# A two-layer conv and attention trunk: layer 1's up projections in seven products of halves, attention in steps of two query blocks

## The chip, the cores and the metric

The kernel runs on one core of a Trainium2 chip. The metric is the device time of one execution in microseconds (us). The engines named below are TensorE (PE in the profile, with PEld for its weight loads), VectorE (DVE), ScalarE (ACT), GpSimd (POOL) and SyncE (SP, which issues DMAs).

## What is computed

The input is 512 tokens of 1024 values in float32. Layer 0 is a causal convolution module (projection and gate, 31 taps per channel, a norm over channels, projection) and a SwiGLU feed-forward block of width 2816. Keys and values are then projected once. Layer 1 is attention (16 heads of 64, four key heads, a window of 128 tokens, a position bias and a sink per head) and a second feed-forward block. A last RMSNorm ends it. The parts that matter here:

```python
def swiglu_ffn(x, w_up, w_down):
    gate, up = jnp.split(x @ w_up, 2, axis=-1)
    return (jax.nn.silu(gate) * up) @ w_down

h = h + attn @ w_o[j]
h = h + swiglu_ffn(rmsnorm(h, norm_ffn[l]), ffn_w_up[l], ffn_w_down[l])
```

In attention each block of 128 queries sees its own block of keys and the one before.

## The kernel before

Values stand channels first: the residual h is eight tiles of 128 channels x 512 tokens. A float32 product is made in three passes (mm3, L268 to L274): every operand is split into a rounded high part and a low remainder, and high x high, high x low and low x high are added up in a PSUM bank. There are eight banks, and bank() (L176) takes the next.

**The weight stream.** Weights come in chunks of 128 x 1024 (512 KB) in the order of PLAN. load (L194) issues their DMAs on SP into four raw buffers; advance (L202) splits them three chunks ahead of their use: a cast on ScalarE to the high part whi and a subtraction on VectorE to the low part wlo (both L214), with four buffers each. get (L254) hands a chunk out.

**The feed-forward block of layer 1.** Its 22 column tiles of gate and up are taken in 11 pairs. A pair (ffn_up, L518) uses four chunks (two halves of the 1024 inputs, gate and up), eight tiles of 128 x 128 each, in three passes over all 512 tokens: 96 matmuls into four banks. evac (L522, L553 to L556) multiplies by the reciprocal norm on VectorE, takes SiLU on ScalarE, multiplies gate by up on GpSimd and splits the result (L430, L431). After the pairs of one part come its down chunks (down_group, L449), 24 matmuls each, and four residual additions per group (L514). The parts are pairs 0 to 5, 6 to 8 and 9 to 10 (HALVES1, LAST); the last part's down products are made token block by token block, from L1156 on. The normalised input comes from Next.on_h (L602): each finished tile of h is multiplied by its gain and split (L426, L427), and its square is added to a sum on GpSimd (Rms.add, L377 to L383).

**Attention.** query (L1020) projects a quarter of the queries. unit (L1040) does two pairs of heads for one block of 128 queries, in stages: scores (one tiny matmul at L1053, then L1057), bias, sink and maximum on VectorE (L1060), exponential on ScalarE (L1067), division on GpSimd (L1071), transposes (L1079) with copies to SBUF (L1081), weighted values (L1088), split (L1094, L1095). pipeline (L1098) has 20 steps over 16 units; each step works on up to four units, and query and the first half of the output projection call a step after each few matmuls. The position bias of all heads stands in one tile, filled by eight DMAs (read_bias, L957). The output projection's second half runs after it, and its residual additions (L1130) feed Next.on_h.

The order of each engine's queue is set by a scheduler from a modelled timeline in which the program's order gives priority; issue_after adds an order by hand. [...] The functions that change:

## Time and profile before

| | |
|---|---|
| median of 3 runs | 1094.72 us (1093.32 to 1095.68) |
| profiled execution | 1092.52 us |
| its span | 1090.7 us |
| granted TensorE clock | 0.999 |
| 580.9 to 720.5 us of the span | queries, attention, output projection |
| 720.5 to 1058.6 us | layer 1's feed-forward block, but for the last down products |

In a row of the timeline stand the start in us from the span's start, the duration, the engine, the line, the operation, what it writes and reads with shapes, how often (x), and in brackets the idle time before it and what ended it. A group's row has the count behind the x, then the busy time in us, the mean of one in ns, and the idle time before the group's instructions. A row of the chain has a start, a duration and the work that the end waited for.

### The profile page before, as it was taken

What the parts mean: (1) busy time and instruction counts of PE and PEld (TensorE: products, weight loads), DVE (VectorE), ACT (ScalarE), POOL (GpSimd) and SP (SyncE); (2) the same over time, 40 slices, a digit from 0 to 9 for tenths busy, and PEclk for the clock granted to TensorE, in tenths of its full rate; (3) what the DMA queues carried; (4) which work ended last, traced back from release to release, by engine and by line L of the source; (5) the groups of instructions that cost most, each with busy time, mean ns of one, the idle gap of its engine ahead of it and who ended that gap; (6) DMA issues with size and microseconds to landing.
All of it is one profiled execution on the core that took longest, in us unless ns stands there. A gap on an engine that the chain in (4) does not pass through costs nothing.

```text
span 1090.7 us, 14781 instructions
## 1 busy us (share of the span) xinstructions
PE 1083.0 (99%) x5514; PEld 910.6 (83%) x5514; DVE 636.8 (58%) x1042; ACT 492.6 (45%) x891; POOL 329.8 (30%) x430
## 2 busy tenths in 40 slices
PE   9999999999999999999999999999999999999997
PEld 8888889999888888888888766788888888888886
DVE  3999988977777554443474666484544333444353
ACT  3887888664655332322353555253322211232233
POOL 3999997710322111110120433050211100111010
PEclk9999999999999999999999999999999999999999
DMA  9247045575566423323222111222222232332212
GB/s 359 75 106 89 20 151 197 183 241 183 186 181 190 142 85 110 96 98 99 97 82 97 58 40 42 90 98 81 97 97 97 97 98 97 97 97 97 97 37 78
DMA packets 39555, 124.39 MB, mean 114 GB/s; under 512 B 4251, under 2 KB 10556, under 8 KB 39484
## 3 DMA queue, kind: packets, MB, share of 16 engines
q1 hardware_dynamic: 38764, 122.36, 35.4%
q10 hardware_dynamic: 720, 1.10, 0.3%
q8 instruction: 43, 0.70, 0.3%
q14 instruction: 28, 0.23, 0.1%
HBM read 118.20 MB, written 5.24 MB: 113 GB/s over the span
## 4 chain that ended last, share of the span: by engine, by line
PE 98%; issue 1%; DMA 0%; POOL 0%; ACT 0%; SPq 0%; POOLq 0%; DVE 0%
PE bank L272 23%; PE bank L273 23%; PE bank L274 23%; PE bank L669 10%; PE bank L304 5%; PE bank L270 4%; PE bank L305 3%; PE bank L1166 2%; PE bank L1088 1%; PE bank L1057 1%; PE bank L1079 1%; PE bank L767 1%; PE bank L657 1%; DMA both<-in_lead_dram 0%; PE bank L419 0%
## 5 line engine op out<-in xcount | busy, mean ns | idle before, releaser
L272 PE MATMUL bank<-quad,whi 128*128 128x512 f32 (+1 forms) x1200 | 440.5, 368 | 0.0
L274 PE MATMUL bank<-quad,wlo 128*128 128x512 f32 (+1 forms) x1200 | 439.1, 366 | 0.0
L273 PE MATMUL bank<-quad,whi 128*128 128x512 f32 (+1 forms) x1200 | 439.0, 366 | 0.0
L214 DVE TENSOR_TENSOR wlo<-raw,whi 128x1024 fp32r<-128x1024 f32 x186 | 258.1, 1388 | 303.8 <-ACT whi L214 299.4
L214 ACT CAST whi<-raw 128x1024 fp32r<-128x1024 f32 x186 | 195.1, 1049 | 326.5 <-PE bank L273 275.1
L272 PEld LDWEIGHTS bank<-quad,whi 128*128 128x128 f32 x1200 | 226.3, 189 | 40.7 <-issue 3.6
L273 PEld LDWEIGHTS bank<-quad,whi 128*128 128x128 f32 x1200 | 226.4, 189 | 37.0 <-issue 1.6
L274 PEld LDWEIGHTS bank<-quad,wlo 128*128 128x128 f32 x1200 | 226.3, 189 | 36.7 <-issue 0.6
L556 POOL TENSOR_TENSOR tmp<-tmp,tmp 128x512 f32<-128x512 f32 x34 | 48.1, 1417 | 408.7 <-DVE tmp L555 393.4
L711 POOL TENSOR_TENSOR pr<-pr,pr 128x256 f32<-128x256 f32 x208 | 156.7, 789 | 7.3 <-ACT pr L710 7.1
L718 DVE SCALAR_TENSOR_TENSOR bank<-apad,wdw,bank 128x256 f32<-128x256 f32 x248 | 112.5, 485 | 3.4
L710 ACT ACTIVATE pr<-apad,wdw 128x256 f32<-128x256 f32 x208 | 98.2, 501 | 14.8 <-POOL pr L711 12.9
L669 PE MATMUL bank<-quad,w 128*128 128x256 f32 x448 | 98.7, 380 | 0.0
L669 PEld LDWEIGHTS bank<-quad,w 128*128 128x128 f32 x448 | 84.9, 190 | 11.8 <-issue 0.2
L383 POOL TENSOR_TENSOR tmp<-tmp,tmp 128x256 f32<-128x256 f32 (+1 forms) x35 | 38.6, 1104 | 154.2 <-ACT tmp L379 117.3
L304 PE MATMUL bank<-quad,whi 128*128 128x512 f32 x212 | 75.9, 398 | 0.0
L554 ACT ACTIVATE tmp<-tmp 128x512 f32<-128x512 f32 x34 | 21.4, 632 | 93.0 <-DVE tmp L553 93.0
L305 PE MATMUL bank<-quad,wlo 128*128 128x256 f32 x212 | 59.3, 280 | 0.0
L1071 POOL TENSOR_SCALAR sc<-sc,sm 128x256 f32<-128x256 f32 (+1 forms) x64 | 32.9, 533 | 71.2 <-DVE sm L1069 71.2
L304 PEld LDWEIGHTS bank<-quad,whi 128*128 128x128 f32 x212 | 39.7, 188 | 8.4
L555 DVE TENSOR_TENSOR tmp<-bank,rsbc 128x512 f32<-128x512 f32 x34 | 23.5, 691 | 32.4 <-PE bank L274 32.4
L1067 ACT ACTIVATE sc<-sc,m 128x257 f32<-128x257 f32 (+1 forms) x64 | 30.2, 473 | 26.4 <-DVE m L1060 20.8
(166 smaller groups left out, 937.5 us busy)
## 6 DMA issues: line engine op xcount, KB each, us to landing
raw<-in_W_dram SPq DMA_DIRECT2D x198, 512.0 KB, 3.5
w<-in_W_dram SPq DMA_DIRECT2D x14, 512.0 KB, 9.6
fd<-fs SPq DMA_DIRECT2D x1, 3072.0 KB, 34.2
h<-in_xT_dram SPq DMA_DIRECT2D x8, 256.0 KB, 8.4
bias<-fd SPq DMA_DIRECT2D x8, 256.0 KB, 5.8
both<-in_lead_dram SPq DMA_DIRECT2D x3, 512.0 KB, 6.0
out_dram<-hg SPq DMA_DIRECT2D x4, 256.0 KB, 2.0
out_dram<-hg ACTq DMA_DIRECT2D x4, 256.0 KB, 2.3
```

What stands on the lines that cost most here:

```text
L214: latest[:] = [nc.scalar.copy(hi, r).ins, lo_engine[0].tensor_sub(lo, r, f32(hi)).ins]
L270: nc.tensor.matmul(out, w[0], x, start=start, stop=stop)
L272: nc.tensor.matmul(out, w[0], x[0], start=start, stop=False)
L273: nc.tensor.matmul(out, w[0], x[1], start=False, stop=False)
L274: nc.tensor.matmul(out, w[1], x[0], start=False, stop=stop)
L304: nc.tensor.matmul(first[2], first[0], first[1], start=start, stop=False)
L305: nc.tensor.matmul(second[2], second[0], second[1], start=False, stop=stop)
L556: nc.gpsimd.tensor_mul(t2, t1, t2)
L669: mm = nc.tensor.matmul(self.pb[:, w * W2:(w + 1) * W2], w1_of(ct, w, k), x[k] if x else xg[k][:, tok], start=k == 0, stop=k == KT - 1)
L710: on_act = nc.scalar.mul(pr, a[:, j:j + W2], tap(j))
L711: on_pool = nc.gpsimd.tensor_add(pr, acc, pr)
L718: on_dve = nc.vector.scalar_tensor_tensor(yt if i == nd - 1 else c, src, tap(i), c if i else self.shift, op0=ALU.mult, op1=ALU.add)
```

## The change

Layer 1's up projections are made by Strassen's method. Weights of a pair are cut in two column tiles and two halves of the inputs, activations in two halves of the inputs and two halves of the tokens, and seven products of halves replace eight. The sums of weights (S1 to S4) are made on GpSimd from the raw chunks and split like a chunk; three pieces (A11, A12, A22) are split directly, gate and up apart. A piece is 1024 columns wide and has 24 matmuls of 256 tokens. The sums of activations (T1 to T4) are made once, by class Rows, while the output projection ends. Products are put together in an SBUF tile (c) by VectorE, GpSimd and ScalarE, before the reciprocal norm. Layer 1 has parts of 4, 3, 2 and 2 pairs instead of 6, 3 and 2. Attention takes two blocks of queries in a step, ten steps instead of twenty; on TensorE each step's matmuls are chained (scores, weighted values, transposes), and the bias stands in tiles by four heads, three buffers, the last filled in the third query. Low parts of weights go behind the last bias operation on VectorE.

```diff
-HALVES1 = ((0, 6), (6, 9))
+HALVES1 = ((0, 4), (4, 7), (7, 9))
...
+SEVEN = ("A11 B11", "S3 T3", "S1 T1", "S2 T2", "A12 B21", "S4 B22", "A22 T4")
+SEVEN_FIRST = ("A11 B11", "S1 T1", "S3 T3", "S2 T2", "A12 B21", "S4 B22", "A22 T4")
...
+def slot_plan(plan):
+
+    slots = []
+    for i, c in enumerate(plan):
+        if c[0] != "up" or not by_seven(c[1], c[2]):
+            slots.append((i, None))
+        elif c[3:] == (0, 0):
+            slots += [(i + (3 if n else 1), (c[1], c[2], n)) for n in range(7)]
+    return slots
...
+    def split_weights(hi, lo, src):
+        on_act = nc.scalar.copy(hi, src).ins
+
+        with tc.issue_after(biased[0]) if biased[0] else nullcontext():
+            latest[:] = [on_act, lo_engine[0].tensor_sub(lo, src, f32(hi)).ins]
...
+    def seven_sources(layer, pair, n):
+
+        name = order_of(layer, pair)[n].split()[0]
+        if name[0] == "S":
+            sums[name] = sums_pool[0].tile([P, 2, 4, P], F32, tag="sum", name=uid("sum"), bufs=4)
+        out = []
+        for which in range(2):
+            a = {f"A{m + 1}{half + 1}": raws[AT["up", layer, pair, half, which]].rearrange("p (k m c) -> p m k c", k=4, m=2)[:, m]
+                 for half in range(2) if n or not half for m in range(2)}
+            if name in a:
+                out.append(a[name])
+                continue
+            s = {k: v[:, which] for k, v in sums.items()}
+            if name == "S1":
+                nc.gpsimd.tensor_add(s[name], a["A21"], a["A22"])
+            elif name == "S2":
+                nc.gpsimd.tensor_sub(s[name], s["S1"], a["A11"])
+            elif name == "S3":
+                nc.gpsimd.tensor_sub(s[name], a["A11"], a["A21"])
+            else:
+                nc.gpsimd.tensor_sub(s[name], a["A12"], s["S2"])
+        return out or [sums[name].rearrange("p a k c -> p (a k c)")]
...
+        load(SLOTS[min(len(SLOTS) - 1, u + SPLIT_AHEAD - 1)][0] + 1 + DMA_AHEAD - SPLIT_AHEAD)
+        while stream["split"] < min(len(SLOTS), u + SPLIT_AHEAD):
+            n = stream["split"]
+            i, blocks = SLOTS[n]
...
+            if blocks is None:
+                split_weights(hi, lo, raws.pop(i))
+                continue
+            src = seven_sources(*blocks)
+            if len(src) == 1:
+                split_weights(hi, lo, src[0])
+                continue
+            for e in range(2):
+                split_weights(*(w[:, e * 512:(e + 1) * 512].rearrange("p (k c) -> p k c", k=4) for w in (hi, lo)), src[e])
...
-        hid = ffn_up(layer, lo, hi, xg, tok, rms, twin, plain)
+        hid = ffn_up7(layer, lo, hi, xg, pool7) if layer else ffn_up(layer, lo, hi, xg, tok, rms, twin, plain)
...
+    class Rows:
+
+
+        def __init__(self, gain):
+            self.gain = gain
+            self.rms = Rms(new_bc(), ALL)
+            self.x = [quad(F32) for _ in range(2)]
+            self.block = {}
+
+        def part(self, name, k, src):
+
+            if name not in self.block:
+                self.block[name] = quads.tile([P, 2, 4, 256], F32R, tag="quad", name=uid("rows"))
+            split([self.block[name][:, a, k:k + 2, :] for a in range(2)], src)
+
+        def on_h(self, i):
+            nc.scalar.mul(self.x[i // 4][:, i % 4, :], h[i], col(self.gain, i))
+            if i < 4:
+                self.rms.add(h[i])
+            if i % 2 == 0:
+                return
+            k = i % 4 - 1
+            b11, b12, b21, b22 = (x[:, k:k + 2, s] for x in self.x for s in HALF)
+            if i < 4:
+                self.part("B11", k, b11)
+                t1 = temp().rearrange("p (k s) -> p k s", k=2)
+                nc.vector.tensor_sub(t1, b12, b11)
+                self.part("T1", k, t1)
+                return
+
+            nc.vector.tensor_sub(b12, b22, b12)
+            self.part("T3", k, b12)
+            nc.vector.tensor_add(b11, b12, b11)
+            self.part("T2", k, b11)
+            self.part("B21", k, b21)
+            if i < 7:
+                return
+            for j in range(4, KT):
+                self.rms.add(h[j])
+            for k in (0, 2):
+                self.part("B22", k, self.x[1][:, k:k + 2, HALF[1]])
+            for k in (0, 2):
+
+                t4 = self.x[1][:, k:k + 2, HALF[0]]
+                nc.gpsimd.tensor_sub(t4, t4, self.x[0][:, k:k + 2, HALF[0]])
+                self.part("T4", k, t4)
+
+    def ffn_up7(layer, lo, hi, rows, pool):
+        hid = Act(2 * (hi - lo))
+        rms = rows.rms
+        for pair in range(lo, hi):
+
+            c = pool.tile([P, 2, 2, 2, 256], F32, tag="up", name=uid("up"), bufs=2)
+            c11, c12, c21, c22 = (c[:, m, s] for m in range(2) for s in range(2))
+            acc = {}
+            for n, name in enumerate(order_of(layer, pair)):
+                w = get_seven(layer, pair, n)
+                a, b = name.split()
+                x = rows.block[b]
+                r = acc[a] = bank().rearrange("p (a s) -> p a s", a=2)
+                for which in range(2):
+                    for k in range(4):
+                        mm3(r[:, which], [v[:, which, k, :] for v in w], [x[:, e, k, :] for e in range(2)],
+                            which == 0 and k == 0, which == 1 and k == 3)
+                if a == "A11":
+                    nc.scalar.copy(c11, r)
+                elif a == "S1":
+                    nc.scalar.copy(c22, r)
+                elif a == "S2":
+                    nc.vector.tensor_add(c12, r, c11)
+                    nc.vector.tensor_add(c21, acc["S3"], c12)
+                    nc.gpsimd.tensor_add(c12, c12, c22)
+                    nc.gpsimd.tensor_add(c22, c21, c22)
+                elif a == "A12":
+                    nc.vector.tensor_add(c11, r, c11)
+                elif a == "S4":
+                    nc.vector.tensor_add(c12, r, c12)
+                elif a == "A22":
+                    nc.vector.tensor_add(c21, r, c21)
+                if pair == 0 and n == 4:
+                    rms.step1()
+            rs_bc = rms.step2().rearrange("p (s q) -> p s q", s=2).unsqueeze(2).to_broadcast([P, 2, 2, 256])
+            for m in range(2):
+                nc.vector.tensor_mul(c[:, m], c[:, m], rs_bc)
+                gate = c[:, m, :, 0, :]
+                nc.scalar.activation(gate, gate, AF.Silu)
+                t = temp()
+                nc.gpsimd.tensor_mul(t.rearrange("p (s q) -> p s q", s=2), gate, c[:, m, :, 1, :])
+                split(hid[2 * (pair - lo) + m], t)
+        return hid
...
+    def read_bias(gp, jp):
+        bias[gp, jp] = at.tile([P, 4, BAND], F32, tag="bias", name=uid("bias"), bufs=3)
+        for g in range(2):
             yield
...
+                        if on_step is not None and n == 7:
                             on_step()
...
+        def pair(gp, jp, n0):
+
+            units = []
+            for n in (n0, n0 + 1):
+                k0 = max(n - 1, 0) * P
+                units.append((n, k0, 1 if n == 0 else 2))
...
+            scs, m4s, all_pbs = [], [], []
+            for _ in units:
+                sc = at.tile([P, 4, 1 + BAND], F32, tag="sc", name=uid("sc"), bufs=4)
+                nc.gpsimd.tensor_copy(sc[:, :, 0].rearrange("p (g e) -> p g e", g=2), sinks4)
+                scs.append(sc)
+                m4s.append(small.tile([P, 4], F32, tag="m4", name=uid("m4")))
+                all_pbs.append([bank().rearrange("p (a b) -> p a b", a=2) for _ in range(2)])
+
+            mm = nc.tensor.matmul(all_pbs[0][1][0:1, 0, 0:1], ones_b, ones_b, start=True, stop=True)
+            for (n, k0, nk), pbs in zip(units, all_pbs):
+                w = nk * P
+                for e in range(2):
+                    for g in range(2):
+                        with tc.issue_after(mm.ins):
+                            mm = nc.tensor.matmul(pbs[g][:, e, 0:w], qs[gp, jp][rows[g], e, n * P:(n + 1) * P],
+                                                  kq[rows[g], gp, k0:k0 + w], start=e == 0, stop=e == 1)
+            for (n, k0, nk), pbs, sc, m4 in zip(units, all_pbs, scs, m4s):
+                w = nk * P
+                for u, hd in enumerate(heads):
+                    biased[0] = nc.vector.tensor_tensor_reduce(
+                        sc[:, u, 1:1 + w], pbs[u // 2][:, u % 2, 0:w], bias[gp, jp][:, u, BAND - w:BAND],
+                        op0=ALU.add, op1=ALU.min, scale=1.0, scalar=sk[:, hd:hd + 1],
+                        accum_out=m4[:, u:u + 1]).ins
+            last_mm[0] = mm
             yield
...
             yield
             pts = []
+            mm = last_mm[0]
+            for (n, k0, nk), sc in zip(units, scs):
+                for kb_ in range(nk):
+                    pt = bank()
+                    for j in range(4):
+                        with tc.issue_after(mm.ins):
+                            mm = nc.tensor.transpose(pt[:, j * P:(j + 1) * P], sc[:, j, 1 + kb_ * P:1 + (kb_ + 1) * P], ident)
+                    pr = at.tile([P, 512], F32, tag="prt", name=uid("prt"), bufs=4)
+                    (nc.vector.tensor_copy if kb_ else nc.scalar.copy)(pr, pt)
+                    pts.append(pr)
+            last_mm[0] = mm
             yield
+            po = bank().rearrange("p (u c) -> p u c", u=2)
+            mm, pts = last_mm[0], iter(pts)
+            for u, (n, k0, nk) in enumerate(units):
+                for kb_ in range(nk):
+                    blk, pr = k0 // P + kb_, next(pts)
+                    for g in range(2):
+                        with tc.issue_after(mm.ins):
+                            mm = nc.tensor.matmul(po[g * HD:(g + 1) * HD, u, :], vq[:, blk, gp, g, :], pr[:, g * BAND:(g + 1) * BAND],
+                                                  start=u == 0 and kb_ == 0, stop=u == 1 and kb_ == nk - 1)
+            last_mm[0] = mm
+            if n0 == 0:
                 os_[gp, jp] = quad()
+            qt = slice(n0 * P, (n0 + 2) * P)
+            src = po.rearrange("p u (j q) -> p j u q", j=2)
+            hi, lo = (os_[gp, jp][:, 2 * a:2 * a + 2, qt].rearrange("p j (u q) -> p j u q", u=2) for a in range(2))
             nc.scalar.copy(hi, src)
             nc.vector.tensor_sub(lo, src, f32(hi))
             yield
 
+        last_mm = [None]
+
         def pipeline():
+            pairs = [pair(gp, jp, n0) for gp in range(2) for jp in range(2) for n0 in (0, 2)]
+            for t in range(len(pairs) + 2):
+                for d in (0, 2, 1, 0):
+                    if 0 <= t - d < len(pairs):
+                        next(pairs[t - d])
...
             next(pipe, None)
 
         for gp, jp in ((0, 1), (1, 0), (1, 1)):
+            if (gp, jp) == (1, 0):
+                drain(read_bias(1, 1))
             query(gp, jp, step)
         for part in range(2):
             for g in range(2):
+                def heads_of(kt):
+                    return tuple(os_[part, kt // 2][:, 2 * a + kt % 2, :] for a in range(2))
+
+                if part == 0:
+
+                    ws = [get("o", kp, g) for kp in range(2)]
+                    banks = {}
+                    for m0, kp in ((0, 0), (0, 1), (2, 0), (2, 1)) if g else ((0, 0), (2, 0), (0, 1), (2, 1)):
+                        order = [(k, m) for k in range(2) for m in (m0, m0 + 1)]
+                        if kp:
+                            order = [(k, m) for m in (m0, m0 + 1) for k in range(2)]
+                        for k, m in order:
+                            if m not in banks:
+                                banks[m] = bank()
+                            mm3(banks[m], [w[:, k, m * P:(m + 1) * P] for w in ws[kp]], heads_of(2 * kp + k),
+                                kp == 0 and k == 0, kp == 1 and k == 1)
+                            if kp and k:
+                                nc.vector.tensor_add(h[g * 4 + m], banks[m], h[g * 4 + m])
+                        if (g, m0, kp) in ((0, 0, 1), (1, 0, 0), (1, 2, 0), (1, 2, 1)):
+                            step()
+                    continue
...
+                    nxt.on_h(i)
             if part == 0:
                 drain(pipe)
+                attn.close()
+                seven = ExitStack()
+                pool7 = sums_pool[0] = seven.enter_context(tc.tile_pool(name="seven", bufs=2))
+                nxt = Rows("ffn1")
...
+    for part in range(len(HALVES1)):
+        ffn_part(1, part, nxt, ALL, None)
+
+    hid = ffn_up7(1, *LAST, nxt, pool7)
+    seven.close()
```

More of the change, by code (lines that the diff above doesn't have):

```diff
@@ L1 @@
 from contextlib import ExitStack, nullcontext
+from itertools import chain
 import numpy as np
@@ L48, with by_seven, order_of, ups @@
 NPARAM = _c
+SEVEN = ("A11 B11", "S3 T3", "S1 T1", "S2 T2", "A12 B21", "S4 B22", "A22 T4")
+SEVEN_FIRST = ("A11 B11", "S1 T1", "S3 T3", "S2 T2", "A12 B21", "S4 B22", "A22 T4")
+def by_seven(layer, pair):
+    return layer == 1
+def order_of(layer, pair):
+    return SEVEN_FIRST if pair == 0 else SEVEN
+def ups(layer, pair):
+    return [("up", layer, pair, half, which) for half in range(2) for which in range(2)]
+def slot_plan(plan):
[6 more added lines that the diff above has]
+    return slots
 def chunk_plan():
@@ L60, in ffn @@
         for pair in range(lo, hi):
-            for half in range(2):
-                for which in range(2):
-                    plan.append(("up", layer, pair, half, which))
+            plan.extend(ups(layer, pair))
         for g in range(2):
@@ L81, in chunk_plan @@
                 plan.append(("o", part * 2 + kp, g))
-    ffn(1, *HALVES1[0])
-    ffn(1, *HALVES1[1])
+    for part in HALVES1:
+        ffn(1, *part)
     for pair in range(*LAST):
-        for half in range(2):
-            for which in range(2):
-                plan.append(("up", 1, pair, half, which))
+        plan.extend(ups(1, pair))
     for kp in range(*LAST):
@@ L964, in hybrid_trunk @@
     base = seen[0]
-    job(read_bias(), (base, 0), (base + 30, 9))
+    job(chain(*(read_bias(*b) for b in ((0, 0), (0, 1), (1, 0)))), (base, 0), (base + 30, 7))
     n1 = Next(("ffn0",), x0, bc0, HALF[1])
@@ L1053, in unit @@
-            mm = nc.tensor.matmul(pbs[1][0:1, 0, 0:1], ones_b, ones_b, start=True, stop=True)
-            for e in range(2):
-                for g in range(2):
-                    with tc.issue_after(mm.ins):
-                        mm = nc.tensor.matmul(pbs[g][:, e, 0:w], qs[gp, jp][rows[g], e, qt], kq[rows[g], gp, k0:k0 + w],
-                                              start=e == 0, stop=e == 1)
-            for u, hd in enumerate(heads):
-                nc.vector.tensor_tensor_reduce(
-                    sc[:, u, 1:1 + w], pbs[u // 2][:, u % 2, 0:w], bias[:, hd, BAND - w:BAND],
-                    op0=ALU.add, op1=ALU.min, scale=1.0, scalar=sk[:, hd:hd + 1],
-                    accum_out=m4[:, u:u + 1])
@@ new lines, in pair @@
+            last_mm[0] = mm
+            yield
+            for (n, k0, nk), sc, m4 in zip(units, scs, m4s):
+                w = nk * P
+                sm = small.tile([P, 4], F32, tag="sm", name=uid("sm"))
+                for j in range(4):
+                    nc.scalar.activation(sc[:, j, 0:1 + w], sc[:, j, 0:1 + w], AF.Exp, bias=m4[:, j:j + 1],
+                                         scale=-1.0, accum_out=sm[:, j:j + 1])
+                nc.vector.reciprocal(sm, sm)
+                for j in range(4):
+                    nc.gpsimd.tensor_scalar(sc[:, j, 1:1 + w], sc[:, j, 1:1 + w], sm[:, j:j + 1], 0.0,
+                                            op0=ALU.mult, op1=ALU.add)
```

83 lines of the change are left out of this document (19 added, 64 removed).

## The prediction

> **What bounds the kernel now.** The page comes first: busy shares, and the chain that ended last.
>
> ```profile
> span 1090.7 us, 14781 instructions
> ...
> PE 1083.0 (99%) x5514; PEld 910.6 (83%) x5514; DVE 636.8 (58%) x1042; ACT 492.6 (45%) x891; POOL 329.8 (30%) x430
> ...
> PE 98%; issue 1%; DMA 0%; POOL 0%; ACT 0%; SPq 0%; POOLq 0%; DVE 0%
> ```
>
> The chain runs through matmuls for 98% of the span: TensorE bounds the kernel, and VectorE (DVE) and GpSimd (POOL) have slack on average. A busy PE is not a PE at its peak, so what a matmul costs is read from the distance between starts. In the timeline of PE, layer 1's up projections issue matmuls of 512 columns, and layer 0's projections over one half of the tokens issue the same three passes with 256:
>
> ```profile
> 800.10 0.39 PE L273 MATMUL bank<-quad,whi 128*128 128x512 f32 x1
> ...
> 811.88 0.39 PE L274 MATMUL bank<-quad,wlo 128*128 128x512 f32 x1
> ```
>
> ```profile
> 225.06 0.28 PE L272 MATMUL bank<-quad,whi 128*128 128x256 f32 x1
> ...
> 229.86 0.28 PE L273 MATMUL bank<-quad,whi 128*128 128x256 f32 x1
> ```
>
> Between the first two lie 52 matmuls: 11.78 / 52 = 0.2265 us each. Between the other two lie 40: 4.80 / 40 = 0.1200 us. Half the columns cost 53% of the time, not 50%.
>
> Next, the limits of the two stages that change, again from PE's timeline.
>
> ```profile
> 580.91 0.40 PE L272 MATMUL bank<-quad,whi 128*128 128x512 f32 x1
> ...
> 731.40 0.95 PE L393 MATMUL bank<-ones_c,tmp 128*128 128x1 f32 x8
> ...
> 1059.63 0.60 PE L1156 MATMUL bank<-ident,h 128*128 128x128 f32 x4
> ```
>
> The first is the first query matmul; the second stands behind the first two chunks of up weights (48 matmuls, 10.9 us), so the output projection ends at 720.5. From there to the third, 339.1 us, PE runs layer 1's feed-forward: 11 pairs x 96 x 0.2265 = 239.2 us up, and 18 chunks x 24 x 0.2265 = 97.8 us down. That is 337.0: PE waits for nothing there. The attention stage takes 139.6 us, of which 384 matmuls of 512 are 87.0; attention's own matmuls take 52.6.
>
> **The change: fewer columns on TensorE.** A pair goes from 96 matmuls of 512 to 7 x 8 x 3 = 168 of 256: 21.74 us becomes 168 x 0.1200 = 20.16. Eleven pairs: **-17.4 us**. Bounds are narrow, since both kinds are in the trace.
>
> **The price: seven pieces of weight, and sums on GpSimd.** Before, a pair split 4 chunks (a cast on ScalarE and one subtraction on DVE). Now there are 7 pieces of the same size; four of them are sums, each two GpSimd operations of 512. After the products come two additions on GpSimd (c12, c22), five DVE additions that read a PSUM bank, two DVE multiplications of 1024, two GpSimd products and two split subtractions of 512. On GpSimd that makes 12 operations of 512 a pair instead of 2; on DVE, subtractions and multiplications with both operands in SBUF: four splits and two multiplications of 1024, and eight operations of 512 (three direct pieces are split in halves, plus the two hidden splits).
>
> What these cost together is read from DVE and POOL side by side, in layer 1:
>
> ```profile
> 764.21 1.29 POOL L556 TENSOR_TENSOR tmp<-tmp,tmp 128x512 f32<-128x512 f32 x1 [13.47 <-DVE tmp L555]
> 766.90 1.60 POOL L556 TENSOR_TENSOR tmp<-tmp,tmp 128x512 f32<-128x512 f32 x1 [1.40 <-DVE tmp L555]
> ```
>
> ```profile
> 763.96 0.68 DVE L553 TENSOR_TENSOR tmp<-bank,rsbc 128x512 f32<-128x512 f32 x1
> ...
> 767.27 2.31 DVE L214 TENSOR_TENSOR wlo<-raw,whi 128x1024 fp32r<-128x1024 f32 x1
> 769.51 0.68 DVE L431 TENSOR_TENSOR quad<-tmp,quad 128x512 fp32r<-128x512 f32 x1
> 772.41 1.23 DVE L214 TENSOR_TENSOR wlo<-raw,whi 128x1024 fp32r<-128x1024 f32 x1 [2.22 <-ACT whi L214]
> ```
>
> The split subtraction takes 1.23 us alone and 2.31 when a GpSimd operation started before it: the second operation waits for the first to end. L553, whose one operand is a PSUM bank, is not held up (0.68) beside the GpSimd operation at 764.21. So DVE operations on two SBUF operands and GpSimd operations take turns. How much a turn takes is seen where they alternate:
>
> ```profile
> 714.52 1.09 DVE L427 SCALAR_TENSOR_TENSOR quad<-h,prm,quad 128x512 fp32r<-128x512 f32 x1
> 715.54 2.31 DVE L214 TENSOR_TENSOR wlo<-raw,whi 128x1024 fp32r<-128x1024 f32 x1
> 717.77 1.77 DVE L427 SCALAR_TENSOR_TENSOR quad<-h,prm,quad 128x512 fp32r<-128x512 f32 x1
> 719.47 0.68 DVE L1130 TENSOR_TENSOR h<-bank,h 128x512 f32<-128x512 f32 x1
> ```
>
> ```profile
> 713.25 5.75 POOL L383 TENSOR_TENSOR tmp<-tmp,tmp 128x512 f32<-128x512 f32 x3 [27.95 <-ACT tmp L379]
> ```
>
> From the end of the first L427 (715.61) to the end of L214 (717.85) one GpSimd operation and one subtraction of 1024 fit in 2.24 us. I take 1.14 for a GpSimd turn, 1.10 for a DVE turn of 1024 and 0.55 for one of 512 (each a little under its row alone, since starts overlap). A pair then needs
>
> - splits: 8 x 1.14 + 4 x 1.10 + 6 x 0.55 = 16.8 us,
> - what follows the products: 4 x 1.14 + 2 x 1.10 + 2 x 0.55 = 7.9 us,
>
> **24.7 us of turns against 20.16 us of matmuls.** Before, it was 2 x 1.14 + 4 x 1.10 + 2 x 0.55 = 7.8 against 21.74. A stage whose cover was wide becomes one where the cover is gone.
>
> [...]
>
> How much of the deficit reaches PE depends on the lead. Pieces are split three ahead, and in a part's down chunks the turns are nearly free, so three products are ready (A11, S3, S1: 1.1 + 3.4 + 3.4 = 7.9 us) when a later part starts. Its first pair keeps up (16.8 < 20.16) and gains no more lead. What follows a part's last pair runs under the down chunks.
>
> - Part 1, four pairs, has no lead. The new normalised halves (class Rows) add 20 DVE turns of 512, seven sums of squares and two differences on GpSimd: 11.0 + 10.3 = 21.3 us; with 4 x 16.8 + 3 x 7.9 = 90.9 that is 112.2 before the last product. From the first residual addition that feeds them (one group, 10.9 us, before the output projection ends) PE's own time is 10.9 + 4 x 20.16 - 2.88 = 88.7. Wait: **+23.5**. The old kernel is already late here: the fifth residual addition runs at 719.47, although its matmuls end 4.1 us before 720.5 (18 more follow); it had 10.9 us of first-half chunks as cover, the new one 5.8 (the first two products).
> - Part 2, three pairs: the last two need 2 x 16.8 - 7.9 + 2 x 7.9 = 41.5 against 2 x 20.16 - 2.88 = 37.4: **+4.1**.
> - Parts of two pairs: 16.8 - 7.9 + 7.9 = 16.8 against 17.3: nothing. But the last pair's hidden rows must be there after one down chunk (24 x 0.2265 = 5.4 us), and the path behind the last product is longer than before: an addition 0.69, a multiplication 1.23, and
>
> ```profile
> L554 ACT ACTIVATE tmp<-tmp 128x512 f32<-128x512 f32 x34 | 21.4, 632 | 93.0 <-DVE tmp L553 93.0
> L430 ACT CAST quad<-tmp 128x512 fp32r<-128x512 f32 x34 | 21.2, 622 | 26.6 <-POOL tmp L556 26.6
> ```
>
>   0.63, 1.29, 0.62 and 0.68 make 5.1, and a turn 6.3: **+2** for both.
> [...]
>
> Together +33.6; the bounds are 12 (S3's and S2's sums made early, both queues well ordered) and 52.
>
> ScalarE's seven casts (1.05 each at most) and the rest stay near 12 us a pair: hidden. Weight loads are the same 44 chunks; eight more residual additions of 0.69 (three parts instead of two) lie under down chunks. The last bias load waits on SP for the first pair of blocks, and weight loads stand behind it; four chunks in buffers cover this, at most 5 us if not.
>
> **Attention by two blocks.** Multiplications and rows are the same; what goes is changes between kinds of matmul on PE. From the chain, in order of time:
>
> ```profile
> 604.08 0.43 PE bank L272
> 604.51 0.23 PE bank L273
> ...
> 607.04 0.44 PE bank L1079 x4
> ...
> 612.26 0.58 PE bank L1088 x4
> ...
> 613.96 0.65 PE bank L1057 x8
> ...
> 624.21 1.01 PE bank L1088 x8
> 625.23 1.02 PE bank L1079 x8
> 626.34 1.06 PE bank L1057 x8
> ```
>
> A full unit is 1.01 + 1.02 + 1.06 = 3.09, a first block 0.44 + 0.58 + 0.65 = 1.67; 12 and 4 of them make 43.8 of the 52.6 us. The other 8.8 are entries, exits (a projection matmul behind attention takes 0.43 instead of 0.23) and broken runs (two runs of L1088 x4 are 1.16, one of x8 1.01). Ten steps instead of twenty, with each step's matmuls in one chain, and eight dummies fewer: between 0 and 9 us saved, I take **-6.4**.
>
> [...]
>
> **Sum**: the profiled execution took 1092.52 us (span 1090.7 and 1.8 around it). 1092.5 - 17.4 - 6.4 + 33.6 = 1102.3. The median of the runs shown lies 2.2 above the profiled execution, so **1104 us**.
>
> **Rivals.** (1) *The turns are absorbed*: work behind the products is put off past the part's end, early sums are made under the output projection, and PE stays the bound. For it: before, PE never waits in this stage, and DVE and GpSimd alone are each under 20 us a pair. Against: 24.7 > 20.16 counts each turn at its shortest. It decides in favour of the change once the waits stay under 21.6 us. With none: 1094.7 - 17.4 - 6.4 = 1071; with half, 1085. Chance 0.22. (2) *Attention loses to PSUM.* A step wants 4 score banks, 1 for the weighted values and 4 for transposes, beside 2 of the projection: 11 of 8. Transposes then wait for the bias step on DVE:
>
> ```profile
> L1060 DVE CUSTOM_DVE_ANT_0 sc<-bank,bias,sk 128x256 f32<-128x256 f32 x48 | 20.4, 479 | 4.1 <-PE bank L1057 4.1
> ...
> L1060 DVE DVE_READ_ACCUMULATOR2_ANT m<- 128x1 f32 x64 | 5.2, 82 | 0.0
> ```
>
> 0.56 us x 4 frees two banks, 8 x 0.56 = 4.5 all; less 1.0 of other PE work that is 1.2 to 3.5 us over 8 steps, 10 to 28. Against: projection matmuls can be ordered in between. With 19 lost in place of 6.4 gained: 1129. Chance 0.12. (3) *The gain isn't there*: matmuls of 256 spaced by their weight load (0.19 us) would cost 168 x 0.19 = 31.9 a pair and 1200 us in all. The rows at 225 to 230 speak against it: 0.03.
>
> My forecast (waits of 20 to 50 us, 1091 to 1120) has 0.63. A measurement of this kernel tells about 0.2%, 2.2 us, from no change. Faster: rival 1 and a little of the forecast's lower end, 0.25; within: 0.09; slower: 0.66. The range takes in half of rival 1 and the lower half of rival 2: 1081 to 1128.
>
> **What would show it.** Right: in layer 1's up stages the distance of 256-column starts stays 0.120, but PE waits for the low weights; split subtractions of about 2.3 us and GpSimd sums of 1.3 to 2.2 alternate without gaps; PE's waits are longest in the first part and nearly absent in the last two. Attention's stage ends about 6 us sooner. Wrong: PE without gaps from 714 on (rival 1), or long waits of transposes for the bias step (rival 2), or split subtractions that stay at 1.23 beside GpSimd sums.

## The result and the profile after

The changed kernel takes **1101.86 us** (median of 5 runs, 1100.67 to 1104.69) against 1094.72 for the kernel before (5 runs, 1093.32 to 1096.5): a ratio of 1.0066, 95% interval 1.0047 to 1.0085. It is slower by 0.7%. The profiled execution took 1101.14 us.

The page of the changed kernel, in the lines shown of before: the span, the busy shares, the chain.

```profile
span 1099.2 us, 16701 instructions
...
PE 1069.2 (97%) x6298; PEld 943.4 (86%) x6298; DVE 767.8 (70%) x1153; ACT 540.7 (49%) x985; POOL 527.9 (48%) x542
...
PE 82%; POOL 8%; DVE 4%; issue 3%; DMA 1%; ACT 1%; SPq 0%; POOLq 0%; DVEq 0%
```

In the last line "issue" is time in which an engine waited for nothing that the profile shows, and a q behind an engine's name stands for its queue. TensorE did 98% of the chain before; now it does 82%, GpSimd 8% and VectorE 4%, though these two are busy only 48% and 70% of the span. Where they entered the chain is seen stage by stage. The columns are the stretch and its length, then busy time (and instructions) of PE, PEld, DVE, ACT and POOL, the granted clock, the DMA share and GB/s. The four stretches are the up projections of the four parts, ideally 80.6, 60.5, 40.3 and 40.3 us.

```profile
710.03:817.10 107.07, 91.80 (x684) 88.50 (x683) 94.19 (x90) 51.81 (x79) 73.51 (x44) 0.94 0.21 72
860.62:928.20 67.58, 63.25 (x505) 61.93 (x504) 50.48 (x50) 29.25 (x43) 42.43 (x24) 0.97 0.24 82
961.10:1001.70 40.60, 40.56 (x337) 40.33 (x336) 29.25 (x31) 18.77 (x27) 21.22 (x12) 1.00 0.26 82
1027.40:1068.00 40.60, 40.56 (x337) 40.34 (x336) 29.26 (x31) 18.77 (x27) 21.16 (x12) 1.00 0.21 78
```

The loss lies in the first stretch (26.4 us over the ideal, about 2 of them the norm's own matmuls) and the second (7.1); the last two run as TensorE could. In the first stretch DVE and POOL are together busy 94 + 74 = 168 us in 107, much of it time in which one holds up the other. The same in POOL's and DVE's rows of the timeline, second pair:

```profile
742.28 1.29 POOL L254 TENSOR_TENSOR sum<-raw,raw 128x512 f32<-128x512 f32 x1
743.53 2.27 POOL L771 TENSOR_TENSOR up<-up 128x512 f32<-128x512 f32 x1
745.77 2.28 POOL L260 TENSOR_TENSOR sum<-raw,sum 128x512 f32<-128x512 f32 x1
748.00 2.28 POOL L256 TENSOR_TENSOR sum<-sum,raw 128x512 f32<-128x512 f32 x1
```

```profile
742.68 1.97 DVE L782 TENSOR_TENSOR up<-up,rsbc 128x1024 f32<-128x1024 f32 x1 [0.90 <-ACT rsbc L490]
744.68 2.21 DVE L236 TENSOR_TENSOR wlo<-sum,whi 128x1024 fp32r<-128x1024 f32 x1
746.81 0.68 DVE L777 TENSOR_TENSOR up<-bank,up 128x512 f32<-128x512 f32 x1
747.52 1.61 DVE L782 TENSOR_TENSOR up<-up,rsbc 128x1024 f32<-128x1024 f32 x1
```

The last three GpSimd operations start 2.24 and 2.23 us apart, with a DVE operation of 1024 between each two; the first, which has the shared time to itself, takes 1.29 and is followed after 1.25. The addition with a PSUM bank (L777, 0.68) runs beside GpSimd unhindered.

How full the shared time is can be counted from both engines' rows. In part 1's second, third and fourth pair GpSimd, or VectorE with an operation that reads no bank, is at work in 22.9 of 24.2 us, 25.5 of 26.7 and 23.5 of 24.8: nearly always.

What PE waits for, first where part 1 begins, in PE's timeline and DVE's:

```profile
710.03 0.28 PE L349 MATMUL bank<-rows,whi 128*128 128x256 f32 x1
...
717.12 0.38 PE L349 MATMUL bank<-rows,whi 128*128 128x256 f32 x1 [1.18 <-ACT rows L507]
720.91 0.38 PE L350 MATMUL bank<-rows,whi 128*128 128x256 f32 x1 [3.40 <-DVE rows L508]
```

```profile
715.80 1.17 DVE L731 TENSOR_TENSOR quad<-quad 128x512 f32<-128x512 f32 x1
716.89 2.29 DVE L236 TENSOR_TENSOR wlo<-sum,whi 128x1024 fp32r<-128x1024 f32 x1
719.10 1.75 DVE L508 TENSOR_TENSOR rows<-quad,rows 128x512 fp32r<-128x512 f32 x1
```

After two products, PE waits for T3's halves: 3.40 us for a row split that stands behind a weight split of 2.29 on DVE and takes 1.75 itself instead of 0.68. The view of waits from 705 to 1070 us (total, times, longest) names the rest, and a second cause:

```profile
POOL sum L254 <- DMA raw<-in_W_dram: 65.0, 9, 19.8
...
PEld bank L351 <- DVE wlo L236: 13.8, 13, 2.2
...
PE bank L351 <- DVE wlo L236: 11.0, 9, 2.0
```

PE waits for low weights. GpSimd, the engine said to be short of time, stands idle 65 us for raw chunks. The longest pieces, 19.8 and 14.9 us, lie at the starts of parts 2 and 4, where products are ready and PE doesn't wait; within part 1 they are 7.8, 5.4 and 5.3 us, before the sums of the second, third and fourth pair. The last of the four raw buffers comes free only when A22, the last product's piece, is split: in the second pair its two splits end at 760.56 and 761.16, and the next loads go out at 760.59 and 761.35.

Attention, in the chain: the scores and weighted values of a step with two full blocks, and 16 transposes of a later step in one run:

```profile
645.11 1.93 PE bank L1234 x16
647.03 1.88 PE bank L1276 x16
...
681.32 1.90 PE bank L1263 x16
```

Its stage runs from 580.5 to 710.0: 129.5 us instead of 139.6.

### The profile page after: what moved, and what is told of

The parts are those of the page before. It is cut to its first block, busy times and chain, and to the rows that moved or that the text cites. A ratio compares the mean times of both kernels' runs of the same rounds, so it can differ in the third digit from the quotient of the medians.

```text
span 1099.2 us, 16701 instructions
## 1 busy us (share of the span) xinstructions
PE 1069.2 (97%) x6298; PEld 943.4 (86%) x6298; DVE 767.8 (70%) x1153; ACT 540.7 (49%) x985; POOL 527.9 (48%) x542
## 4 chain that ended last, share of the span: by engine, by line
PE 82%; POOL 8%; DVE 4%; issue 3%; DMA 1%; ACT 1%; SPq 0%; POOLq 0%; DVEq 0%
PE bank L351 18%; PE bank L350 18%; PE bank L349 18%; PE bank L837 9%; PE bank L381 5%; PE bank L347 4%; PE bank L382 3%; DVE wlo L236 2%; POOL sum L256 2%; POOL sum L254 2%; PE bank L1380 1%; PE bank L1234 1%; PE bank L1276 1%; PE bank L1263 1%; POOL sum L260 1%
## 5 line engine op out<-in xcount | busy, mean ns | idle before, releaser
L236 DVE TENSOR_TENSOR wlo<-raw,whi 128x1024 fp32r<-128x1024 f32 (+1 forms) x208 | 263.4, 1278 | 162.6 <-ACT whi L233 162.4
L350 PE MATMUL bank<-quad,whi 128*128 128x512 f32 (+1 forms) x848 | 302.0, 356 | 1.8 <-DVE quad L508 1.8
L233 ACT CAST whi<-raw 128x1024 fp32r<-128x1024 f32 (+1 forms) x208 | 186.0, 911 | 236.7 <-PE bank L350 171.7
L351 PE MATMUL bank<-quad,wlo 128*128 128x512 f32 (+1 forms) x848 | 301.9, 356 | 0.0
L349 PE MATMUL bank<-quad,whi 128*128 128x512 f32 (+1 forms) x848 | 300.8, 357 | 1.1 <-ACT quad L507 1.1
L351 PE MATMUL bank<-rows,wlo 128*128 128x256 f32 x616 | 177.8, 290 | 11.1 <-DVE wlo L236 11.0
L349 PE MATMUL bank<-rows,whi 128*128 128x256 f32 x616 | 178.1, 290 | 5.2 <-ACT whi L233 4.0
L349 PEld LDWEIGHTS bank<-quad,whi 128*128 128x128 f32 x848 | 160.2, 189 | 25.4 <-ACT quad L507 1.9
L350 PEld LDWEIGHTS bank<-quad,whi 128*128 128x128 f32 x848 | 160.4, 189 | 24.9 <-DVE quad L508 2.8
L350 PE MATMUL bank<-rows,whi 128*128 128x256 f32 x616 | 177.3, 288 | 3.4 <-DVE rows L508 3.4
L351 PEld LDWEIGHTS bank<-quad,wlo 128*128 128x128 f32 x848 | 160.3, 189 | 22.9 <-issue 0.6
L351 PEld LDWEIGHTS bank<-rows,wlo 128*128 128x128 f32 x616 | 120.7, 196 | 13.8 <-DVE wlo L236 13.8
L349 PEld LDWEIGHTS bank<-rows,whi 128*128 128x128 f32 x616 | 121.0, 197 | 7.1 <-ACT whi L233 5.3
L350 PEld LDWEIGHTS bank<-rows,whi 128*128 128x128 f32 x616 | 121.0, 197 | 4.1 <-DVE rows L508 3.8
L878 ACT ACTIVATE pr<-apad,wdw 128x256 f32<-128x256 f32 x208 | 98.2, 501 | 14.9 <-POOL pr L879 12.9
L236 DVE TENSOR_TENSOR wlo<-sum,whi 128x1024 fp32r<-128x1024 f32 x44 | 71.0, 1614 | 43.9 <-ACT whi L233 43.8
```

The source lines that it names most:

```text
L233: on_act = nc.scalar.copy(hi, src).ins
L236: latest[:] = [on_act, lo_engine[0].tensor_sub(lo, src, f32(hi)).ins]
L349: nc.tensor.matmul(out, w[0], x[0], start=start, stop=False)
L350: nc.tensor.matmul(out, w[0], x[1], start=False, stop=False)
L351: nc.tensor.matmul(out, w[1], x[0], start=False, stop=stop)
L878: on_act = nc.scalar.mul(pr, a[:, j:j + W2], tap(j))
```

## The experiments

Two theories at first. **Turns**: low parts and GpSimd's sums exclude each other, and the two queues are late. **Late loads**: the sums begin late because raw chunks come late. The experiments change the kernel after unless said otherwise; each is timed beside the kernel before, and its ratio is to that. Differences in us between two of these kernels are of medians from different sets; by the ratios those to the kernel after are up to 1.4 us smaller.

**Attention alone.** Layer 1's feed-forward as before, attention by two blocks.

```diff
-HALVES1 = ((0, 4), (4, 7), (7, 9))
+HALVES1 = ((0, 6), (6, 9))
...
-    return layer == 1
+    return False
```

> Layer 1's up projections as before (four chunks, 96 matmuls of 512, parts of 6, 3 and 2 pairs), attention by two blocks kept. The stage from the first query matmul to the end of the output projection fell from 139.6 to 129.5 us in the changed kernel. If that gain is attention's own, the time is 1094.7 - 10 = about 1085 us and PE waits for nothing in layer 1's feed-forward block (339 us). If it hangs on the first products that follow it, the time is 1090 or more.

Measured: 1082.75 us, ratio 0.9906 (0.9891 to 0.9921). Attention's 10 us are there without the products. Its groups carry them, as read in the chain of the kernel after: 44 us of attention matmuls before became four times (1.51 + 1.45 + 1.46 for a first step, 1.93 + 1.88 + 1.90 for a second) = 40.5, and entries, exits and broken runs 2.0 instead of 8.8. The clock stays at 1.000.

**Low parts without turns.** The low part is formed against a PSUM bank of zeros, so it is the whole value, and it no longer waits for the cast; the output differs by that.

```diff
-            latest[:] = [on_act, lo_engine[0].tensor_sub(lo, src, f32(hi)).ins]
+            nc.vector.tensor_sub(lo, src, zero[0]...)
```

> The low part of the seven pieces is formed against a PSUM bank of zeros instead of the high part in SBUF, so it is the whole value and not the remainder; one bank fewer for the rest. GpSimd does the same 12 operations a pair. Turns theory (operations of VectorE on two SBUF operands and operations of GpSimd exclude each other): 24.7 us of turns a pair become about 17, under PE's 20.2, and most of the 36 us of waits go: 1070 to 1078 us, split subtractions near 1.2 us beside GpSimd sums. If the waits come from chunks that are loaded late, or from GpSimd's own speed, the time stays over 1093.

Measured: 1071.78, ratio 0.9804 (0.9788 to 0.9821). Parts 2 to 4 have no wait at all (60.47, 40.31, 40.31), part 1 takes 88.5. The group of low parts of sums in the kernel after, then in this one (from 705 to 1070 us):

```profile
L236 DVE TENSOR_TENSOR wlo<-sum,whi 128x1024 fp32r<-128x1024 f32 x44 | 71.0, 1614 | 43.9 <-ACT whi L233 43.8
```

```profile
L243 DVE TENSOR_TENSOR wlo<-sum,bank 128x1024 fp32r<-128x1024 f32 x43 | 52.3, 1216 | 38.3 <-PE bank L359 10.7 <-POOL sum L268 8.4 <-POOL sum L264 7.1
```

and DVE beside POOL:

```profile
758.65 1.22 DVE L243 TENSOR_TENSOR wlo<-sum,bank 128x1024 fp32r<-128x1024 f32 x1 [0.72 <-POOL sum L262]
```

```profile
757.32 1.30 POOL L262 TENSOR_TENSOR sum<-raw,raw 128x512 f32<-128x512 f32 x1
758.57 1.30 POOL L778 TENSOR_TENSOR up<-up 128x512 f32<-128x512 f32 x1
759.84 1.30 POOL L268 TENSOR_TENSOR sum<-raw,sum 128x512 f32<-128x512 f32 x1
```

GpSimd goes on at 1.27 us a piece while the low part takes 1.22. The two no longer meet, and 30 us are gone. This edit also takes away DVE's wait for the cast; the next ones, which keep it, say how much the turns alone bear.

**A fifth raw buffer**, one chunk more of loads ahead.

```diff
+            if sums_pool[0] is not None and i % 5 == 0:
+                r = sums_pool[0].tile([P, 1024], F32, tag="fifth", name=uid("raw"), bufs=1)
```

> Five raw buffers for chunks in layer 1 instead of four, loads requested one chunk earlier; all operations as in the changed kernel. GpSimd is idle there for 5.3 us before the first sum of half of the pairs while a chunk is loaded. Turns theory: turns are the same 24.7 us, the gain is 0 to 4 us (1098 to 1102). Late loads theory: waits at each change of pair go, 10 us or more (under 1092).

Measured: 1095.88, ratio 1.0024 (1.0012 to 1.0035): 6 us less than after. This is between the theories: late loads are a cause. How large a one isn't settled by this run, since GpSimd still waits 5.4, 2.5 and 4.6 us for chunks before the three pairs' sums in part 1, where it waited 7.8, 5.4 and 5.3.

**Fewer turns: products put together on VectorE.** The two additions and the gate product go from GpSimd to DVE (24.7 us of turns a pair become 24.7 - 4 x 1.14 + 4 x 0.55 = 22.3).

```diff
-                    nc.gpsimd.tensor_add(c12, c12, c22)
+                    nc.vector.tensor_add(c12, c12, c22)
...
-                nc.gpsimd.tensor_mul(t..., gate, c[:, m, :, 1, :])
+                nc.vector.tensor_mul(t..., gate, c[:, m, :, 1, :])
```

> The product of gate and up and the two additions c12 and c22 move from GpSimd to VectorE; nothing else changes. Turns theory: four turns of 1.14 become four of 0.55, 24.7 becomes 22.3 us a pair, 7 us less wait in part 1 and up to 5 in part 2: 1090 to 1095 us. Late loads theory: within 2 us of 1101.9. If VectorE's own work is the bound (16 us a pair becomes 18.7), the time grows to over 1104.

Measured: 1090.73, ratio 0.9977 (0.9967 to 0.9987). As the turns theory said: 11 us, in part 1 (100.5) and part 2 (63.0). GpSimd's waits for raw chunks grew meanwhile (L254 73.0 us and L258 63.6, where they were 65.0 and 10.0), so they aren't by themselves what PE pays for. The edit also shortens GpSimd's own queue by four of twelve operations; with low parts against a bank GpSimd kept all twelve, and the waits behind the first pair went all the same.

**One operand in PSUM.** The norm factor and the product S1 stay in their banks, and the gate product goes into a bank: 17.9 us of turns a pair.

```diff
-                elif a == "S1":
-                    nc.scalar.copy(c22, r)
...
-                    nc.gpsimd.tensor_add(c22, c21, c22)
+                    nc.vector.tensor_add(c22, acc["S1"], c21)
...
-                t = temp()
+                t = bank()
...
```

> All the kernel's work, with fewer turns: the factor of the norm and the S1 product stay in PSUM banks, c12 and c22 and the product of gate and up are VectorE's, the latter into a bank. GpSimd keeps the eight sums a pair. Turns theory: 8 x 1.14 + 4 x 1.10 + 6 x 0.55 + 2 x 0.55 = 17.9 us a pair, under PE's 20.2; what is left is part 1's start, as when the low parts were formed against a bank (1071.8): 1072 to 1080 us. VectorE-bound theory (its own operations come to 17 to 19 us a pair): no better than 1090.7 with the post work on VectorE.

Measured: 1085.56, ratio 0.9924 (0.9912 to 0.9937). Better again, but the expectation is missed: turns below the 20.16 us of matmuls don't end the waits. Part 1 still takes 97.1, part 2 62.2, and the down chunks of part 3 25.3 instead of 21.7.

**The same with the fifth buffer.**

> The same with a fifth raw buffer in layer 1. Turns theory: late loads matter only while the turns are short of time, so 0 to 2 us less than with four buffers. Late loads as a cause of their own: again 6 us less.

Measured: 1082.60, ratio 0.989 (0.9874 to 0.9906). Part 2 reaches 60.5, part 1 94.7.

**The same with the gate product on GpSimd again**, so 20.2 us of turns; the 19.1 expected below leaves the two hidden splits (2 x 0.55) out of the sum.

> As the one before, but the product of gate and up on GpSimd again (into SBUF): 2 x 1.14 instead of 2 x 0.55, and two split subtractions again on two SBUF operands: 19.1 us of turns a pair. Turns theory: still under 20.2, so 0 to 4 us slower than the one before, all of it in part 1.

Measured: **1078.18**, ratio 0.9856 (0.9841 to 0.9872), faster where the expectation was slower: the down chunks of part 3 take 21.8 us again instead of 24.2, so the last pair's hidden rows come sooner (2.4 of the 2.7 us by which the two profiled executions differ). DVE has less to do behind the last product; that this is why is argued, not isolated. It beats the kernel before, the change and attention alone (0.9891 to 0.9921). Since attention alone brings 0.9% of the 1.4%, the seven products bring 0.5% here, some 5 us of the 17.4 that TensorE saves. Its part 2, by the same columns as above:

```profile
848.20:908.70 60.50, 60.50 (x506) 60.48 (x505) 53.74 (x59) 29.04 (x41) 28.15 (x17) 1.00 0.31 104
```

Part 1 keeps 14 us over the ideal.

**Fillers against the clock.** After the waits at 715 the granted clock falls to 0.50 for 10.2 us (last section). Sixteen matmuls whose result nobody reads stand after the first pair's second product, in the kernel after:

```diff
+                if pair == 0 and n == 1:
+                    spare = bank()
+                    for j in range(16):
+                        nc.tensor.matmul(spare, w[0][:, 0, j % 4, :], ...)
```

> The changed kernel with 16 more matmuls of 512 columns (3.6 us) into a spare bank after the second product of the first pair, where PE waited for 1.5 and 3.8 us and the granted clock was 0.5 for the 10.2 us that followed. If the half clock lies on the path, the 43 matmuls that took 0.213 instead of 0.120 us come back: 4 us less (1098). If turns set the pace of part 1 anyway, the time stays within 2 us of 1101.9 although the clock stays at 1.0.

Measured: 1106.35, ratio 1.0106 (1.0091 to 1.0121). They came on top, and the clock fell later all the same (0.74 over 727 to 740 us).

**The order of the first pair's products**, in the best version: A12 B21 third, B21 split ahead of T3's. The product A12 B21 also enters c12 here, so part of the output differs.

```diff
-SEVEN_FIRST = ("A11 B11", "S1 T1", "S3 T3", "S2 T2", "A12 B21", "S4 B22", "A22 T4")
+SEVEN_FIRST = ("A11 B11", "S1 T1", "A12 B21", "S3 T3", "S2 T2", "S4 B22", "A22 T4")
```

> The kernel with post work in banks, gate on GpSimd and five raw buffers (1078.2), with A12 B21 as third product of the first pair instead of the fifth, and B21 split ahead of T3. In the kernel without this, PE waits 2.2, 2.2 and 2.1 us for T3's halves. Start theory (what is left of part 1's loss is the activations' sums standing in a row on VectorE behind the last residual additions): B21 needs no sum, so 2 to 4 us less, 1074 to 1076. If the split weights still set the pace, no change.

Measured: 1078.11, ratio 0.9854 (0.9839 to 0.9868): no difference. Three waits of 3.0, 1.8 and 2.1 us, from start to start, stand in place of 2.2, 2.2 and 2.1.

**More fillers**, 22 and 10 after the second and third product, in the best version.

> The same kernel (1078.2) with 22 and 10 matmuls of 512 columns (5.0 and 2.3 us) into a spare bank after the second and third product of the first pair, in the place of waits of 4.4 and 2.1 us. There the granted clock was 0.5 for 13.7 us after the waits. If the half clock follows from the waits and lies on the path, it goes away and some 4 us come back: 1074. If fillers only take the place of waits, 1078; if they come on top, up to 1085.

Measured: 1082.08, ratio 0.9892 (0.9875 to 0.9908), 4 us worse. PE then waits 5.05 us in one piece for a split of rows on DVE, and the clock is at half for 6.8 us instead of 13.7.

**Seven products with the old attention.**

> Seven products in layer 1 with the attention of the kernel before (20 steps, one bias tile). If the two parts of the change add up, the time is 1101.9 + 10.5 = 1112 us (attention alone gave 1082.75 against 1093.6 to 1094.7). If the seven products lose only because attention by pairs of blocks delays their start, it is nearer to 1100.

Measured: 1117.05, ratio 1.0214 (1.0198 to 1.0229). The feed-forward stage takes 361.9 us and attention's 139.6. The effects add up to within 5 us; 3.7 of these lie ahead of the first query, in code that nothing here touches.

**Squares late**, in the best version: the last four squares and their sums behind T4, the norm after the first pair's last product.

> The kernel with post work in banks, gate on GpSimd and five raw buffers (1078.2), with the last four squares and their sums on GpSimd put behind the last sums of activations (T4); the norm's sum is taken on TensorE after the first pair's last product. Part 1 still takes 94.4 us instead of 80.6 there, all but 0.5 us of its long waits in the first pair. If GpSimd's turns for these four sums (4.6 us) delay the sums of activations on VectorE, 2 to 4 us come back: 1074 to 1076. If the start is bound by the row of operations on VectorE alone, no change.

Measured: 1088.68, ratio 0.9954 (0.994 to 0.9967), 10.5 us worse. The seven products of the first pair take 31.1 us, hardly less than the 32.6 that they took with the norm among them, so the squares weren't what held them up. The loss is one wait:

```profile
742.51 0.95 PE L473 MATMUL bank<-ones_c,tmp 128*128 128x1 f32 x8
753.99 2.05 PE L499 MATMUL bank<-tmp,ones_m 128*128 128x512 f32 x2 [10.53 <-DVE tmp L480]
```

```profile
740.61 1.30 POOL L257 TENSOR_TENSOR sum<-raw,raw 128x512 f32<-128x512 f32 x1 [2.53 <-DMA raw<-in_W_dram]
...
749.83 1.25 POOL L257 TENSOR_TENSOR sum<-raw,raw 128x512 f32<-128x512 f32 x1
751.05 1.01 POOL L477 TENSOR_TENSOR rs<-ms,mhalf 128x4 f32<-128x4 f32 x1
```

The norm's tiny step on GpSimd (L477), whose input VectorE had ready at 746.58, stands in its queue behind the second pair's sums, two of which wait for raw chunks, and starts at 751.05; PE's own queue holds the norm's matmuls ahead of the second pair.

## Why the prediction was right

It gave 1104 us and slower; 1101.86 was measured. By its own steps, against the profiled 1101.14:

- **Columns, -17.4: right.** Starts in the undisturbed parts lie 0.120 us apart (336 matmuls in 40.31 us in the experiments, 40.60 in the kernel itself). Strassen's saving is real on TensorE. Rival 3 (spacing by the weight load) is refuted.
- **Turns, the mechanism: right.** That the cover is gone, that split and sum alternate (2.24 us a round, as worked out from the rows of before), that the first part suffers most and the last two hardly: the trace shows each. They don't alternate "without gaps", though, as GpSimd waits for raw chunks in between. Fewer turns, where VectorE still waits for the cast, bring 11 and 16 us back, nearly half of the loss; the 30 us with low parts against a bank belong to the turns and to that wait together. Beside GpSimd a low part took 1.22 us with one operand in SBUF (low parts against a bank), against 2.21 with two (the kernel after).
- **Waits, +33.6: measured 36.3** (the stage went from 339.1 to 358.0; -17.4 + 36.3). Part 1: +24 without the norm's matmuls, predicted 23.5. Its pairs stand 9.2 us, 4.0, 6.5 and 4.6 over 20.16; for the last three, 24.7 against 20.16 foretold 4.5 each. Part 2: +7.1, predicted 4.1. Down chunks after the last pairs: +3.9, all in part 3, predicted 2. The remaining 1.3 lie in small pieces. The sum's other 4 us, for queues that stand idle, were the author's estimate, and no run shows that term; measured were 1.3, 1.2 and 1.3 us in part 1's second, third and fourth pair in which neither GpSimd nor a VectorE operation that reads no bank was at work. The sum was near, its composition less so. It left out two things, which overlap with the turns. Raw chunks come late for the sums: the fifth buffer gives 6 us. And matmuls at half clock: in part 1 some 64 starts, most of them in its stretches, lie 0.15 to 0.4 us apart, 6.5 us over 0.120 together.
- **Turns below the matmuls' time end the waits**: this inverse of the argument, on which the expectation of 1072 to 1080 us for one operand in PSUM rests, is wrong as such. At 17.9 us of turns PE still waited; with the fifth buffer as well, part 2 has no wait left (60.5), so late chunks were one reason. Operations that stand behind a waiting one in their queue, as the norm's step under "Squares late" (input ready at 746.58, started at 751.05), may be a second; it was not isolated.
- **Attention, -6.4: too small.** It measured -10.1 and fell outside the bound of 9. The step that was off is the cost of the runs themselves: they were left as they were, but 16 matmuls of a kind in one run are cheaper than two runs of 8 (1.93 against 2.12 for scores, 1.90 against 2.04 for transposes): 3.3 us, beside 6.8 of entries, exits and broken runs.
- **Rival 1** (turns absorbed, 1071 to 1085) didn't happen in this kernel, but the edits of the best version come into its range (1078). Its "with half, 1085" is a slip: half of 33.6 on top of 1071 makes 1088. **Rival 2** (attention loses to PSUM) is refuted: PE is busy 129.53 of the stage's 129.53 us, and attention alone gains.
- **The basis.** 2.2 was added from the profiled execution to the median; after it is 0.7. Together: 1092.5 - 17.4 - 10.1 + 36.3 - 0.4 ahead of the first query = 1100.9. That the sum of 1102.3 came within 1.2 us of the profiled execution is luck in part: 3.7 us too little for attention and 2.7 too little for the waits nearly cancel.

**Open**: what holds up the first pair. In the best version it takes 32.6 us instead of 20.16: three waits that make 6.1 us, 3.5 us more for slow matmuls, and the norm's matmuls with what stands beside them. Order of products, squares and fillers were tried and are not it. What PE waits for there is a cast of rows on ScalarE behind one of weights, a row split on DVE behind a weight split of 2.08 us, and a row split that takes 1.75 us instead of 0.68. With low parts against a bank the first pair takes 27.7 us, so splits of weights bear a part of it; whether by their turns or by VectorE's wait for the cast was not isolated. Nor was it settled whether the half clock itself costs time there, or only fills time in which PE would have waited.

## What to carry to other kernels

Fewer columns on TensorE pay only if the sums that buy them fit on the other engines: where a trace shows DVE operations with two SBUF operands and GpSimd operations taking turns, as here (starts 2.24 us apart instead of 1.25), count them as one queue, and compare it with the matmuls' time pair by pair: 24.7 us against 20.16 left 36.3 us of waits. A sum below that time is no promise that the waits end: 17.9 us against 20.16 still left some. Here an operand left in a PSUM bank took an operation out of that queue (beside GpSimd a low part took 1.22 us so, and 2.21 with both operands in SBUF); such operands, with one more raw buffer, turned 0.7% slower into 1.4% faster. And two edits in one change can hide each other: here attention gained 10 us while the products lost 19.

## What the runs showed of the hardware

The granted clock fell to 0.50 in the middle of a busy kernel. PE in the kernel after, from 720 to 731 us (length, busy, clock), and two neighbours in its timeline:

```profile
720.00:731.00 11.00, 10.09 (x46) 0.56 0.00 0
```

```profile
728.55 0.41 PE L351 MATMUL bank<-rows,wlo 128*128 128x256 f32 x1
728.76 0.41 PE L349 MATMUL bank<-rows,whi 128*128 128x256 f32 x1
```

Starts lie 0.213 us apart instead of 0.120, for 10.2 us from 721.3 on (granted clock 0.50), just after PE had stood nearly idle from 715.7 to 720.9 (busy for 0.62 of 5.20 us); again for 3.4 us at 775.9 (0.50) and at 912.5 (0.51), after waits of 0.8 to 2.0 us. PE's rows ahead of 775.9:

```profile
772.43 0.39 PE L349 MATMUL bank<-rows,whi 128*128 128x256 f32 x1 [0.88 <-ACT whi L233]
774.90 0.39 PE L351 MATMUL bank<-rows,wlo 128*128 128x256 f32 x1 [1.96 <-DVE wlo L236]
```

Up to 1068 us the half clock lasted 10.2 us once and 3.4 us twice in the kernel after; it lasted 6.8 us with more fillers and 13.7 us in the best version, each within 0.1 us of a multiple of 3.4. With attention alone the granted clock of the profiled execution was 1.000. What makes the clock fall was not isolated: the drop at 721.3 came after a wait of 3.40 us, the one at 775.9 after none longer than 1.96 us in the ten us before it.
